# Weight-block sums by adding DMAs, another order of the seven products, and no arithmetic on GpSimd

## Chip, cores and metric

One core of one Trainium2 chip runs the whole program. The metric is device time in microseconds of one execution of the program, as the median of several runs. The profile is of one execution.

## The reference, cut to what matters

Two encoder layers on 512 tokens of width 1024: latent attention in the first, grouped-query attention in the second, each beside a four-head cross-attention into 256 memory tokens, an output projection with residual, and then a SwiGLU block:

```python
def _swiglu(h, w_gate_up, w_down):
    gu = h @ w_gate_up                       # (512, 1024) @ (1024, 2 * 2816)
    g, u = gu[..., :D_FF], gu[..., D_FF:]
    return (jax.nn.silu(g) * u) @ w_down

for i in range(DEPTH):
    ...
    x = x + jnp.concatenate([mix, mem_out], axis=-1) @ w_out[i]
    x = x + _swiglu(_rmsnorm(x, norm_ffn[i]), w_gate_up[i], w_down[i])
```

All weights and activations are float32.

## The kernel before

**Products in three passes.** Every large product is made of float32r matmuls. A weight tile is loaded in float32 (`load_raw`, L166, from SyncE's queue), ACT rounds it to a high half (`whi`, L154 in `wsplit`), DVE subtracts to get the low half (`wlo`, L155), and `mm3` (L137 to L139) issues three matmuls: high by high, high by low, low by high. An activation tile is split in the same way.

**Gate/up in seven products instead of eight** (`ffn`). The reduction (1024) is cut in two halves, the tokens in two halves, and a group of columns holds gate columns and the up columns that belong to them. So a group has four weight blocks: B11 and B21 (gate, upper and lower half of the reduction), B12 and B22 (up), numbered q = 0, 2, 1, 3. Seven products P1 to P7 of sums of A blocks (activations) by sums of B blocks (weights) replace the eight plain ones. There are six groups a layer, five 512 columns wide (each block two tiles of 128x1024) and a last one 256 wide (each block one tile). A step is one weight tile of one product: twelve matmuls of 512 moving columns, so a full group has 14 steps.

The list `PROD` sets the order of products. `prep(g, p, i)` makes the weight tile of a step; `ahead(n)` calls it two steps ahead of the matmuls (`LW=2`), and the high and low halves lie in three buffers each (`WF=3`). In `prep`, the function `tadd` subtracts in place on DVE (L793): two subtractions for each tile of P7, one for P6, one for P4, so 8 of 128x1024 in a full group. `post(g, p)` takes a product out of PSUM: ACT copies for P1, P7 and P5 (L868, L872, L880), GpSimd adds P7 to P5 (L881) and P6 to that (L886), DVE does the rest (L885, L890, L892, L896, L897). `act_T` transposes a group's result for w_down after the next group's P1. The A sums (`get` in `w_out`, L708) are made once a layer, when the first group needs them.

**w_down** (after the groups): each activation tile is split by ACT (`ah`, L943) and, by turns, DVE and GpSimd (`al`, L944, `wlod='VP'`).

**Elsewhere on GpSimd**: `rope_tables` loads tables with DMAs from GpSimd's queue (L375, L376, L380) and multiplies them there (L386, L387), at the start of the program and at the start of layer 1.

**Order.** The program is written in one order, and a scheduler places each engine's instructions and inserts the semaphore waits. Each engine, and each queue, runs its list in order.

Of the kernel before, what the change touches and what calls it, by code (L numbers as in the profile page):

```python
# [28 lines left out]

CFG = dict(mid=3, mgap=3, mdel=7, warm=9, npre=(3, 3), pre=(6, 5), WC=512, mm=3, sc=3, tp=2, norm='VA', G=33, T=9,  # L30
           W=7, WH=6, WF=3, RF=3, PR=4, delay=12, ssq='AV', ahead=1, gtag=('sc', 'mm', 'mm', 'mm'), LA=3, wlos='V',
           wloa='V', wlof='V', wlod='VP', scl='V', rm='V', rad='V', hi='A', rawe='A', LW=2, tadd='V',
           r=(0.534, 0.925, 0.95, 5, 1.124, 0.86, 1.362))
# [15 lines left out]
def encoder_kernel(ctx: ExitStack, tc: tile.TileContext, a: dict, out: bass.AP):  # L49
# [270 lines left out]
    def w_early(src, n):  # L320

        ws = []
        raw = g4(dt=F32, name="raw")
        nc.sync.dma_start(raw[:, : n * 512], src[:, : n * 512])
        for i in range(n):
            w = pair()
            split(w, raw[:, i * 512 : (i + 1) * 512])
            ws.append(w)
        return ws
# [39 lines left out]
    def rope_tables(cs, rows, row0, d, ntab):  # L369
        t_cs = gt((P, 2, 4, d), F32) if 8 * d <= 512 else None  # L370
        if t_cs is None:
            t_c, t_s = [x.rearrange("p (t d) -> p t d", t=4) for x in pair(F32)]
        else:
            t_c, t_s = t_cs[:, 0], t_cs[:, 1]
        GP.dma_start(t_c, cs[0].rearrange("p (t d) -> p t d", t=4))  # L375
        GP.dma_start(t_s, cs[1].rearrange("p (t d) -> p t d", t=4))  # L376
        out = []
        for i in range(ntab):
            g = tt()[:, : 2 * d]
            GP.dma_start(g, rows[:, row0 + 2 * i * d : row0 + (2 * i + 2) * d])  # L380
# [6 lines left out]
            GP.tensor_mul(sg, t_s, g[:, d : 2 * d].unsqueeze(1).to_broadcast([P, 4, d]))  # L387
            out.append((cg, sg))
        return out
# [293 lines left out]

    def w_out(l, acts, banks, pre, X, g0, early):

# [18 lines left out]
        def sums(x, y, op):  # L704
# [4 lines left out]
            return o  # L709

        def get(name):
            (a11, a21), (a12, a22) = rows
# [4 lines left out]
            if name == "A12":  # L717
                scale_rows(1)
                return operand(a12)
            if name == "S1":  # L720
                tmp["S1"] = sums(a21, a22, V.tensor_add)
                return operand(tmp["S1"])
            if name == "S2":
                tmp["S2"] = sums(tmp["S1"], a11, V.tensor_sub)
                return operand(tmp["S2"])
            if name == "A22":
                return operand(a22)
            return operand(sums(a12, tmp["S2"], V.tensor_sub))

# [8 lines left out]
        for i, (c, kp, ts) in enumerate(steps):  # L738
# [17 lines left out]
            elif (c, kp) == (1, 3):  # L756
                scale_rows(0)
        add_x(X, 1, bs[1], sq, range(4))

        def stats():  # L760
            tot = small(4, "sqt")
            V.tensor_add(tot, sq[:, :4], sq[:, 4:])
            return token_rstd(tot, 4, D, f"rf{l}")[0]

# [3 lines left out]

    PROD = ["P1", "P7", "P2", "P5", "P6", "P4", "P3"]
    AOP = dict(P1="A11", P7="S3", P2="A12", P5="S1", P6="S2", P4="A22", P3="S4")  # L770

    def ffn(l, X, acts, banks, pre, g0, emit):
# [11 lines left out]
        def ntile(g):  # L784
            return 2 if g < 5 else 1

        def load_q(g, q):
            if g < NG:
                src = [a["w_gu"][l, g, q, i] for i in range(2)] if g < 5 else [a["w_gl"][l, q]]
                raws[g, q] = [load_raw(x, 1024) for x in src]  # L790

        def tadd(o, x, y):
            (V if eng("tadd") == "V" else GP).tensor_sub(o, x, y)  # L793

        def prep(g, p, i):
            b11, b12, b21, b22 = [raws[g, q][i] if (g, q) in raws else None for q in range(4)]
            if p == "P1":
                src = b11
            elif p == "P7":
                tadd(b11, b12, b11)  # L800
                tadd(b12, b22, b12)
                src = b12
            elif p == "P2":
                src = b21
            elif p == "P5":
                src = b11
            elif p == "P6":
                tadd(b11, b22, b11)
                src = b11
            elif p == "P4":  # L810
                tadd(b11, b21, b11)
                src = b11
            else:
                src = b22
            return wsplit(src, 1024, "wlof")

# [4 lines left out]
        def ahead(n):  # L821
            while nprep[0] < min(n, len(steps)):
# [16 lines left out]
        def early(get):  # L839
            if getop[0] is None:  # L840
                getop[0] = get
                load_q(0, 0)
                ahead(1)
            else:
                ahead(2)

        stats = w_out(l, acts, banks, pre, X, g0, early)
        st = {}
# [14 lines left out]
        def post(g, p):  # L863
# [5 lines left out]
            elif p == "P7":  # L869
                st["p7"] = two()  # L870
                for t in range(2):
                    A.copy(st["p7"][t][:, :n], st["B"][t])  # L872
            elif p == "P2":
                st["gs"] = [pr(), pr()]
                for t in range(2):
                    A.activation(st["gs"][t][:, :n], st["A"][t], AF.Silu, scale=r[:, t : t + 1])
            elif p == "P5":
                st["p5"] = two()
                for t in range(2):
                    A.copy(st["p5"][t][:, :n], st["C"][t])  # L880
                    GP.tensor_add(st["p5"][t][:, :n], st["p5"][t][:, :n], st["p7"][t][:, :n])  # L881
            elif p == "P6":
                for t in range(2):
                    w, z = st["p1"][t][:, :n], st["p5"][t][:, :n]
                    V.tensor_add(w, st["D"][t], w)  # L885
                    GP.tensor_add(z, z, w)  # L886
            elif p == "P4":
                for t in range(2):
                    w, z, q = [st[x][t][:, :n] for x in ("p1", "p5", "p7")]
                    V.tensor_add(q, st["B"][t], w)  # L890
                    A.activation(q, q, AF.Silu, scale=r[:, 2 + t : 3 + t])
                    V.scalar_tensor_tensor(z, z, r[:, 2 + t : 3 + t], q, ALU.mult, ALU.mult)  # L892
            else:
                for t in range(2):
                    w, q = st["p1"][t][:, :n], st["gs"][t][:, :n]
                    V.tensor_add(w, st["C"][t], w)  # L896
                    V.scalar_tensor_tensor(w, w, r[:, t : t + 1], q, ALU.mult, ALU.mult)  # L897
                return [st["p1"][0], st["p1"][1], st["p5"][0], st["p5"][1]]

# [602 lines left out]
```

## Time and profile before

| | us |
|---|---|
| median of 3 runs | 1308.55 (1307.23 to 1310.11) |
| the profiled execution | 1308.39 |
| its span in the trace | 1306.6 |
| TensorE matmul busy | 1273.2 |
| DVE busy | 945.6 |
| ACT busy | 711.7 |
| GpSimd busy | 155.9 |
| read from HBM | 119.24 MB |

The profile shows engines as PE (TensorE's matmuls), PEld (its weight loads), DVE, ACT, POOL (GpSimd) and SP (SyncE); a q behind a name is the engine's queue or sequencer. L155 is a line of the kernel before. Matmuls are pipelined: 0.39 us is the time of one from its start to its end, while the next begins earlier. The 1.8 us between the profiled execution's time and its span lie around the instructions.

### The profile page before, as it was taken

What the parts mean: (1) busy time and instruction counts of PE and PEld (TensorE: products, weight loads), DVE (VectorE), ACT (ScalarE), POOL (GpSimd) and SP (SyncE); (2) the same over time, 40 slices, a digit from 0 to 9 for tenths busy, and PEclk for the clock granted to TensorE, in tenths of its full rate; (3) what the DMA queues carried; (4) which work ended last, traced back from release to release, by engine and by line L of the source; (5) the groups of instructions that cost most, each with busy time, mean ns of one, the idle gap of its engine ahead of it and who ended that gap; (6) DMA issues with size and microseconds to landing.
All of it is one profiled execution on the core that took longest, in us unless ns stands there. A gap on an engine that the chain in (4) does not pass through costs nothing. (4 is left out here: it accounts for less than half of the span.)

```text
span 1306.6 us, 17197 instructions
## 1 busy us (share of the span) xinstructions
PE 1273.2 (97%) x6425; PEld 1063.0 (81%) x6425; DVE 945.6 (72%) x1591; ACT 711.7 (54%) x1229; POOL 155.9 (12%) x84
## 2 busy tenths in 40 slices
PE   8999999989999999989999999999999999999998
PEld 6988878878878887978888888887887888898887
DVE  6699998735987988962326798965498888888221
ACT  5587776834755455542324478866375555555110
POOL 2000000000312221330100000000013222035000
PEclk9999999989999999999999999999999999999999
DMA  6342101053233231241313212223304133215210
GB/s 224 116 139 85 34 1 49 1 209 113 78 132 129 81 121 46 76 165 49 125 49 113 89 49 70 77 81 113 113 34 176 55 123 113 79 52 186 106 62 33
DMA packets 45027, 122.44 MB, mean 94 GB/s; under 512 B 5217, under 2 KB 9825, under 8 KB 44945
## 3 DMA queue, kind: packets, MB, share of 16 engines
q1 hardware_dynamic: 44352, 119.58, 26.7%
q0 software_dynamic: 592, 1.77, 0.4%
q8 instruction: 50, 0.82, 0.3%
q14 instruction: 33, 0.26, 0.1%
HBM read 119.24 MB, written 2.10 MB: 93 GB/s over the span
## 5 line engine op out<-in xcount | busy, mean ns | idle before, releaser
L155 DVE TENSOR_TENSOR wlo<-raw,whi 128x1024 fp32r<-128x1024 f32 (+3 forms) x342 | 375.3, 1106 | 248.0 <-ACT whi L154 246.1
L154 ACT CAST whi<-raw 128x1024 fp32r<-128x1024 f32 (+3 forms) x342 | 299.2, 885 | 394.0 <-PE sc L139 259.1
L881 POOL TENSOR_TENSOR t<-t,t 128x512 f32<-128x512 f32 (+1 forms) x24 | 65.1, 2733 | 901.1 <-ACT t L880 901.1
L137 PE MATMUL mm<-whi,g 128*128 128x512 f32 (+3 forms) x370 | 141.6, 384 | 1.2 <-ACT whi L154 1.2
L138 PE MATMUL mm<-wlo,g 128*128 128x512 f32 (+3 forms) x370 | 139.8, 378 | 0.5 <-DVE wlo L155 0.5
L139 PE MATMUL mm<-whi,g 128*128 128x512 f32 (+3 forms) x370 | 138.8, 378 | 0.0
L138 PE MATMUL mm<-wlo,op 128*128 128x512 f32 (+1 forms) x336 | 127.3, 379 | 4.3 <-DVE wlo L155 3.8
L137 PE MATMUL mm<-whi,op 128*128 128x512 f32 (+1 forms) x336 | 125.9, 375 | 3.2 <-ACT whi L154 3.2
L139 PE MATMUL mm<-whi,op 128*128 128x512 f32 (+1 forms) x336 | 125.9, 375 | 0.0
L139 PE MATMUL sc<-whi,op 128*128 128x512 f32 (+1 forms) x336 | 125.1, 372 | 0.0
L138 PE MATMUL sc<-wlo,op 128*128 128x512 f32 (+1 forms) x336 | 125.0, 372 | 0.0
L137 PE MATMUL sc<-whi,op 128*128 128x512 f32 (+1 forms) x336 | 124.9, 372 | 0.0
L793 DVE TENSOR_TENSOR raw<-raw,raw 128x1024 f32<-128x1024 f32 x88 | 110.5, 1275 | 1.1
L138 PEld LDWEIGHTS mm<-wlo,op 128*128 128x128 f32 x336 | 63.2, 188 | 21.9 <-DVE wlo L155 11.3
L137 PEld LDWEIGHTS mm<-whi,g 128*128 128x128 f32 x370 | 69.8, 189 | 12.5 <-ACT whi L154 1.6
L138 PEld LDWEIGHTS mm<-wlo,g 128*128 128x128 f32 x370 | 70.2, 190 | 10.5 <-DVE wlo L155 1.0
L139 PEld LDWEIGHTS mm<-whi,g 128*128 128x128 f32 x370 | 69.8, 189 | 10.9 <-DVE g L246 0.2
L137 PEld LDWEIGHTS mm<-whi,op 128*128 128x128 f32 x336 | 63.3, 188 | 14.7 <-ACT whi L154 3.6
L499 PE MATMUL sc<-g,g 128*128 128x512 f32 x256 | 73.6, 403 | 0.6 <-ACT g L243 0.6
L138 PE MATMUL mm<-wlo,ah 128*128 128x512 f32 x176 | 69.0, 392 | 4.3 <-DVE wlo L155 4.3
L138 PEld LDWEIGHTS sc<-wlo,op 128*128 128x128 f32 x336 | 63.3, 188 | 11.2
L139 PEld LDWEIGHTS sc<-whi,op 128*128 128x128 f32 x336 | 63.3, 188 | 11.0
(243 smaller groups left out, 2663.6 us busy)
## 6 DMA issues: line engine op xcount, KB each, us to landing
raw<-in_w_gu SPq DMA_DIRECT2D x80, 512.0 KB, 4.3
raw<-in_w_dn SPq DMA_DIRECT2D x44, 512.0 KB, 3.9
raw<-in_w_out SPq DMA_DIRECT2D x24, 512.0 KB, 4.4
raw<-in_w_mkv SPq DMA_DIRECT2D x32, 256.0 KB, 2.9
raw<-in_w_gin SPq DMA_DIRECT2D x30, 256.0 KB, 3.0
raw<-in_w_gl SPq DMA_DIRECT2D x8, 512.0 KB, 4.0
raw<-in_w_out SPq DMA_DIRECT2D x12, 256.0 KB, 2.5
raw<-in_w_qb SPq DMA_DIRECT2D x12, 192.0 KB, 2.3
```

What stands on the lines that cost most here:

```text
L137: PE.matmul(out, lhi, rhi, start=start, stop=False, skip_group_check=skip)
L138: PE.matmul(out, lhi, rlo, start=False, stop=False, skip_group_check=skip)
L139: PE.matmul(out, llo, rhi, start=False, stop=stop, skip_group_check=skip)
L154: A.copy(hi[:, :n], raw)
L155: (V if eng(kind) == "V" else GP).tensor_sub(lo[:, :n], raw, f(hi[:, :n]))
L499: PE.matmul(sc, lq[:, q * P : (q + 1) * P], rk, start=i == 0, stop=i == len(passes) - 1)
L793: (V if eng("tadd") == "V" else GP).tensor_sub(o, x, y)
L881: GP.tensor_add(st["p5"][t][:, :n], st["p5"][t][:, :n], st["p7"][t][:, :n])
```

## The change

- **Weight sums.** The seven products get signs so that each B sum is a plain addition. The subtractions on DVE (`tadd`, L793) go. In their place GpSimd's queue issues DMAs that read a weight block from HBM a second time and add it into the tile in SBUF (`add_q`, L808 of the new kernel). Tile q = 0 is split for P1, then B12 is added into it and it is split for P5, then B22 (split for P6), then B21 (split for P4). Tile q = 1 gets B22 added before it is split for P7. That is 8 adding DMAs of 512 KB in a full group and 4 in the last group, 88 in all.
- **Order of products.** P1, P7, P5, P2, P6, P3, P4 instead of P1, P7, P2, P5, P6, P4, P3. So the splits of tile q = 0 lie four steps apart (steps 0, 4, 8, 12 of the 14). The A sums change signs to match, and the third product of a layer is S1 (two sums, then splits) instead of A12.
- **Loads.** All loads of the second to fourth block go to the `raw` buffers (four instead of three), those of q = 0 to the general pool (32 slots instead of 33). The first group's loads start two steps of w_out earlier (`first`).
- **GpSimd's arithmetic goes.** The P5 sum is one DVE instruction that reads PSUM (instead of an ACT copy and a GpSimd addition), the P6 sum, all of w_down's `al` and the rope tables' multiplications move to DVE.
- `w_early` loads two tiles of 512 columns apart instead of one of 1024.

```diff
-    ..., G=33, ... RF=3, ... wlod='VP', ...
+    ..., G=32, ... RF=4, ... wlod='V', ...
...
-            GP.tensor_mul(cg, t_c, g[:, :d].unsqueeze(1).to_broadcast([P, 4, d]))
+            V.tensor_mul(cg, t_c, g[:, :d].unsqueeze(1).to_broadcast([P, 4, d]))
...
-    PROD = ["P1", "P7", "P2", "P5", "P6", "P4", "P3"]
+    PROD = ["P1", "P7", "P5", "P2", "P6", "P3", "P4"]
...
+        def add_q(g, q, by, i):
+            if g < NG:
+                GP.dma_start(raws[g, q][i], w_src(g, by)[i], accum_op=ALU.add)
+
+        BOP = dict(P1=(0, 1), P7=(1, None), P5=(0, 3), P2=(2, None), P6=(0, 2), P3=(3, None), P4=(0, None))
+
+        def load_sum(g):
+            load_q(g, 1)
+            for i in range(ntile(g) if g < NG else 0):
+                add_q(g, 1, 3, i)
+
         def prep(g, p, i):
-            b11, b12, b21, b22 = [raws[g, q][i] if (g, q) in raws else None for q in range(4)]
-            if p == "P1":
-                src = b11
-            elif p == "P7":
-                tadd(b11, b12, b11)
-                tadd(b12, b22, b12)
-                src = b12
-...
+            q, by = BOP[p]
+            w = wsplit(raws[g, q][i], 1024, "wlof")
+            if by is not None:
+                add_q(g, q, by, i)
+            return w
...
                 if i == 0:
-                    for q in {"P1": [1, 3], "P7": [2], "P5": []}.get(p, []):
-                        if (g, q) not in raws:
-                            load_q(g, q)
-                    if p == "P6":
+                    if p == "P5":
+                        load_q(g, 2)
+                    elif p == "P2":
+                        load_q(g, 3)
+                    elif p == "P6":
                         load_q(g + 1, 0)
-                    if p == "P3":
-                        load_q(g + 1, 1)
+                    elif p == "P3":
+                        load_sum(g + 1)
...
             elif p == "P5":
                 st["p5"] = two()
                 for t in range(2):
-                    A.copy(st["p5"][t][:, :n], st["C"][t])
-                    GP.tensor_add(st["p5"][t][:, :n], st["p5"][t][:, :n], st["p7"][t][:, :n])
+                    V.tensor_add(st["p5"][t][:, :n], st["C"][t], st["p7"][t][:, :n])
             elif p == "P6":
                 for t in range(2):
                     w, z = st["p1"][t][:, :n], st["p5"][t][:, :n]
                     V.tensor_add(w, st["D"][t], w)
-                    GP.tensor_add(z, z, w)
+                    V.tensor_add(z, z, w)
```

**GpSimd, one full group of layer 0** (`t` are results of products, `raw` weight tiles). Before, the four additions of two tiles each:

```order
L881 TENSOR_TENSOR t_1175_5071<-t_1175_5071,t_1159_4991 128x512
L881 TENSOR_TENSOR t_1176_5072<-t_1176_5072,t_1160_4992 128x512
L886 TENSOR_TENSOR t_1175_5071<-t_1175_5071,t_1145_4927 128x512
L886 TENSOR_TENSOR t_1176_5072<-t_1176_5072,t_1146_4928 128x512
```

Now, tile q = 0 being `raw_1119` and `raw_1120`, and `raw_1189` and `raw_1190` being the next group's q = 1:

```order
L808 DMA raw_1119_4727<-in_w_gu 128x1024
L808 DMA raw_1120_4729<-in_w_gu 128x1024
L808 DMA raw_1119_4727<-in_w_gu 128x1024
L808 DMA raw_1120_4729<-in_w_gu 128x1024
L808 DMA raw_1189_5085<-in_w_gu 128x1024
L808 DMA raw_1119_4727<-in_w_gu 128x1024
L808 DMA raw_1190_5087<-in_w_gu 128x1024
L808 DMA raw_1120_4729<-in_w_gu 128x1024
```

The list holds the additions for P5, P6 and P4 of both tiles, and the next group's sums stand between those for P4, on the same queue.

**DVE around a change of groups in layer 0.** Before, from the last product but one (`mm`, `sc` are PSUM):

```order
L892 SCALAR_TENSOR_TENSOR t_1176_5072<-t_1176_5072,rf0_975_4017,t_1160_4992 128x512
L793 TENSOR_TENSOR raw_1169_5033<-raw_1183_5117,raw_1169_5033 128x1024
L155 TENSOR_TENSOR wlo_1194_5180<-raw_1170_5035,whi_1193_5179 128x1024
L896 TENSOR_TENSOR t_1145_4927<-mm_1167_5031,t_1145_4927 128x512
L896 TENSOR_TENSOR t_1146_4928<-sc_1168_5032,t_1146_4928 128x512
L897 SCALAR_TENSOR_TENSOR t_1145_4927<-t_1145_4927,rf0_975_4017,pr_1165_5027 128x512
L897 SCALAR_TENSOR_TENSOR t_1146_4928<-t_1146_4928,rf0_975_4017,pr_1166_5028 128x512
L793 TENSOR_TENSOR raw_1183_5117<-raw_1189_5159,raw_1183_5117 128x1024
L793 TENSOR_TENSOR raw_1170_5035<-raw_1184_5119,raw_1170_5035 128x1024
L155 TENSOR_TENSOR wlo_1200_5208<-raw_1183_5117,whi_1199_5207 128x1024
```

Now, the same place (the last product is P4, L907 and L909):

```order
L155 TENSOR_TENSOR wlo_1202_5166<-raw_1179_5041,whi_1201_5165 128x1024
L155 TENSOR_TENSOR wlo_1204_5183<-raw_1180_5043,whi_1203_5182 128x1024
L907 TENSOR_TENSOR t_1167_4995<-mm_1159_4955,t_1151_4925 128x512
L907 TENSOR_TENSOR t_1168_4996<-sc_1160_4956,t_1152_4926 128x512
L155 TENSOR_TENSOR wlo_1208_5208<-raw_1189_5085,whi_1207_5207 128x1024
L909 SCALAR_TENSOR_TENSOR t_1177_5037<-t_1177_5037,nr0_978_4025,t_1167_4995 128x512
L909 SCALAR_TENSOR_TENSOR t_1178_5038<-t_1178_5038,nr0_978_4025,t_1168_4996 128x512
L155 TENSOR_TENSOR wlo_1210_5224<-raw_1190_5087,whi_1209_5223 128x1024
```

The first low half of P7 (`wlo_1200` before, `wlo_1208` now) has three subtractions of 128x1024 fewer between it and the end of the old group, and stands ahead of that group's last two instructions.

## Rows read from the trace of the kernel before

**Rows 1.** Windows: gate/up of layer 0, its end, gate/up of layer 1 (stretch and length, busy, clock, DMA share, GB/s).

```profile
340.00:560.00 220.00, 214.66 (x1055) 178.58 (x1054) 192.05 (x185) 123.00 (x161) 55.30 (x25) 1.00 0.30 101
560.00:580.00 20.00, 16.30 (x65) 12.97 (x64) 17.73 (x9) 10.79 (x12) 12.99 (x5) 0.91 0.33 120
960.00:1180.00 220.00, 217.05 (x1062) 180.98 (x1062) 190.99 (x186) 127.17 (x168) 55.08 (x25) 1.00 0.27 94
```

**Rows 2.** Waits of weight loads, 340 to 560 us (who waited for whom: total, times, longest).

```profile
PEld mm L138 <- DVE wlo L155: 6.5, 11, 1.1
PEld mm L137 <- ACT whi L154: 2.1, 1, 2.1
```

**Rows 3.** The same, 960 to 1180 us.

```profile
PEld mm L138 <- DVE wlo L155: 4.9, 10, 1.0
PEld mm L137 <- ACT whi L154: 1.5, 1, 1.5
```

**Rows 4.** The same, 1180 to 1200 us.

```profile
PEld mm L138 <- DVE wlo L155: 1.1, 1, 1.1
```

**Rows 5.** The same, first 30 us.

```profile
PEld sc L139 <- DVE wlo L155: 1.4, 2, 1.2
PEld mm L139 <- DVE wlo L155: 1.1, 2, 0.8
```

**Rows 6.** Timeline of PE where w_down begins, layer 0 (start, duration, instruction, idle before).

```profile
565.19 0.39 PE L137 MATMUL sc<-whi,ah 128*128 128x512 f32 x1
...
566.55 0.39 PE L137 MATMUL mm<-whi,ah 128*128 128x512 f32 x1
570.64 0.50 PE L138 MATMUL mm<-wlo,ah 128*128 128x512 f32 x1 [3.70 <-DVE wlo L155]
...
572.03 0.63 PE L139 MATMUL mm<-whi,al 128*128 128x512 f32 x1
572.46 0.63 PE L137 MATMUL sc<-whi,ah 128*128 128x512 f32 x1
```

**Rows 7.** Timeline of DVE, the same place.

```profile
561.25 6.04 DVE L944 TENSOR_TENSOR al<-at,ah 128x1024 fp32r<-128x1024 f32 x2 [0.67 <-ACT ah L943]
567.21 6.68 DVE L155 TENSOR_TENSOR wlo<-raw,whi 128x1024 fp32r<-128x1024 f32 x2
```

**Rows 8.** Timeline of POOL, the same place.

```profile
560.35 12.46 POOL L944 TENSOR_TENSOR al<-at,ah 128x1024 fp32r<-128x1024 f32 x4 [7.26 <-ACT ah L943]
```

**Rows 9.** Line L155 from 340 to 560 us: duration ns least/median/most.

```profile
L155 DVE TENSOR_TENSOR wlo<-raw,whi x73: 1207/1224/2315, 339.3 to 553.1; 128x1024 fp32r<-128x1024 f32 x73
```

**Rows 10.** Groups of DVE, 340 to 560 us (busy us, mean ns, idle before).

```profile
L155 DVE TENSOR_TENSOR wlo<-raw,whi 128x1024 fp32r<-128x1024 f32 x73 | 99.7, 1383 | 23.7 <-ACT whi L154 23.2
L793 DVE TENSOR_TENSOR raw<-raw,raw 128x1024 f32<-128x1024 f32 x40 | 52.8, 1342 | 0.4
...
L885 DVE TENSOR_TENSOR t<-mm,t 128x512 f32<-128x512 f32 x5 | 3.4, 678 | 0.0
```

**Rows 11.** Line L380, DMAs issued by POOL: time of the issue, ns.

```profile
L380 POOL DMA_DIRECT2D t<-in_rows x4: 534/536/582, 3.8 to 619.9; - x4
```

**Rows 12.** Group of ACT over the span: the high half (busy us, mean ns, idle before).

```profile
L154 ACT CAST whi<-raw 128x1024 fp32r<-128x1024 f32 x220 | 230.0, 1053 | 328.7 <-PE sc L139 211.8 <-DVE raw L793 52.5 <-PE mm L139 34.1
```

**Rows 13.** The profile page, DMA issues (count, KB each, median us from issue to landing).

```profile
raw<-in_w_gu SPq DMA_DIRECT2D x80, 512.0 KB, 4.3
...
g<-in_rope_mla POOLq DMA_DIRECT2D x2, 256.0 KB, 6.2
...
g<-in_rope_gqa POOLq DMA_DIRECT2D x2, 256.0 KB, 2.9
```

**Rows 14.** DMA queues from 400 to 500 us (packets, MB, share of 16 engines).

```profile
q1 hardware_dynamic: 2796, 10.14, 28.9%
```

**Rows 15.** The chain that ended last: one instruction in two groups of layer 1, two groups apart.

```profile
1034.77 1.13 DVE raw L793
...
1115.85 1.13 DVE raw L793
```

More of the change, by code (lines that the diff above doesn't have):

```diff
@@ L322, in w_early @@
         ws = []
-        raw = g4(dt=F32, name="raw")
-        nc.sync.dma_start(raw[:, : n * 512], src[:, : n * 512])
         for i in range(n):
-            w = pair()
-            split(w, raw[:, i * 512 : (i + 1) * 512])
-            ws.append(w)
+            raw, hi, lo = tt(), tt(dt=F32R), tt(dt=F32R)
+            nc.sync.dma_start(raw, src[:, i * 512 : (i + 1) * 512])
+            split((hi, lo), raw)
+            ws.append((hi, lo))
         return ws
@@ L682, in add_x, with w_out @@
             A.activation(tt(), xc, AF.Square, accum_out=sq[:, 4 * c + t : 4 * c + t + 1])
-    def w_out(l, acts, banks, pre, X, g0, early):
+    def w_out(l, acts, banks, pre, X, g0, first, early):
         sq = small(8, f"sq{l}", bufs=1)
@@ L727, in get @@
                 return operand(a22)
-            return operand(sums(a12, tmp["S2"], V.tensor_sub))
+            return operand(sums(tmp["S2"], a12, neg_sum))
         n = len(banks)
@@ L757, in w_out @@
                 scale_rows(0)
+                first()
         add_x(X, 1, bs[1], sq, range(4))
@@ L845, in early, with first @@
                 ahead(2)
-        stats = w_out(l, acts, banks, pre, X, g0, early)
+        def first():
+            load_q(0, 0)
+            load_sum(0)
+        stats = w_out(l, acts, banks, pre, X, g0, first, early)
         st = {}
@@ L872, in post @@
                     A.copy(st["p7"][t][:, :n], st["B"][t])
+            elif p == "P5":
+                st["p5"] = two()
+                for t in range(2):
+                    V.tensor_add(st["p5"][t][:, :n], st["C"][t], st["p7"][t][:, :n])
             elif p == "P2":
@@ L875, in post @@
                 for t in range(2):
[L876 to L879, printed above, removed]
-                    A.copy(st["p5"][t][:, :n], st["C"][t])
-                    GP.tensor_add(st["p5"][t][:, :n], st["p5"][t][:, :n], st["p7"][t][:, :n])
+                    A.activation(st["gs"][t][:, :n], st["A"][t], AF.Silu, scale=r[0][:, t : t + 1])
             elif p == "P6":
@@ L885, in post @@
                     V.tensor_add(w, st["D"][t], w)
-                    GP.tensor_add(z, z, w)
-            elif p == "P4":
+                    V.tensor_add(z, z, w)
+            elif p == "P3":
+                st["p3"] = [pr(), pr()]
+                for t in range(2):
+                    w, q, u = [st[x][t][:, :n] for x in ("p1", "gs", "p3")]
+                    V.tensor_add(u, st["C"][t], w)
+                    V.scalar_tensor_tensor(u, u, r[1][:, t : t + 1], q, ALU.mult, ALU.mult)
+            else:
                 for t in range(2):
@@ L890, in post @@
                     V.tensor_add(q, st["B"][t], w)
[L891 to L898, printed above, removed]
+                    A.activation(q, q, AF.Silu, scale=r[0][:, 2 + t : 3 + t])
+                    V.scalar_tensor_tensor(z, z, r[1][:, 2 + t : 3 + t], q, ALU.mult, ALU.mult)
+                return [st["p3"][0], st["p3"][1], st["p5"][0], st["p5"][1]]
         BANK = dict(P1="A", P7="B", P2="A", P5="C", P6="D", P4="B", P3="C")
```

46 lines of the change are left out of this document (20 added, 26 removed).

## Prediction

> **What bounds the kernel now.** I first cut the span into stages. In gate/up of layer 0 TensorE is busy 214.66 of 220 us, in layer 1 217.05 of 220; DVE is busy 192.05 and 190.99 there, so nearly nine tenths, and GpSimd a quarter [rows 1]. TensorE sets the time, and DVE is the engine that sometimes keeps it waiting. So the change can give back only what TensorE loses, and the next view is who it waits for. Its weight loads wait for low and high halves of weights: 6.5 and 2.1 us in layer 0 [rows 2], 4.9 and 1.5 us in layer 1 [rows 3], 1.1 us where layer 1 goes over to w_down [rows 4], 1.4 and 1.1 us at the program's start [rows 5]. Where layer 0 goes over to w_down, two matmuls start 4.09 us apart (566.55 and 570.64) and the trace names `wlo`; afterwards matmuls start 0.43 us apart instead of 0.23 [rows 6]. The granted clock of that stretch is 0.91 [rows 1]: after the idle gap it fell to 1.2 GHz, and that is 9% of 20 us, 1.8 us more.
>
> Why is `wlo` late? In the last place DVE spends 6.04 us on two `al` and 6.68 us on two `wlo` [rows 7], while GpSimd works on four `al` for 12.46 us [rows 8]. A `wlo` alone takes 1.22 us (median), the longest 2.3 us [rows 9]. So the two engines slow each other, and over gate/up of layer 0 the mean is 1.38 us [rows 10]. The second reason is DVE's own list: 40 subtractions of weight blocks, 52.8 us in five groups [rows 10], stand between the splits.
>
> **What leaves and what comes on the engines.** A full group loses 8 subtractions of 1.34 us on DVE, 10.7 us [rows 10]. It gains four instructions of 512 columns there (the sums for P5 and P6), about 0.68 us each by the row of a like one [rows 10], 2.7 us. If the 73 splits also fall from 1.38 to 1.22 us [rows 9, 10], DVE saves 12 us more over the stretch. So its 192 us become about 192 - 53 + 14 - 12 = 141 of 220. w_down's eleven `al` that move from GpSimd cost DVE about 1.22 us each (priced as a `wlo` of the same size [rows 9]); DVE waits for work in w_down, and the four that lie at the change of stage take the place of two that were stretched to 3 us each. The eight multiplications of the rope tables, 0.68 us each at most, cost DVE under 3 us at each of two starts; in layer 1 they stand behind four splits that are ahead of need, so I cost them at nothing, and at the program's start I keep 1 us for them. The ACT copies for P5 go; ACT is not what is waited for. `w_early` moves the same bytes: nothing.
>
> **What TensorE can get back.** From above, all these waits: 8.6 (layer 0) + 3.9 + 1.8 (end of layer 0, 4.09 less one normal 0.23, and the clock) + 6.4 (layer 1) + 1.1 + 2.5 (start) = 24.3 us [rows 1 to 6]. From below, TensorE's plain idle time by the windows, 5.3 + 3.7 + 2.9, and the clock: 13.8 us [rows 1]; it counts too little, because a matmul's busy time of 0.39 us covers the start of a gap. I take, stage by stage, 6.5 of 8.6, 5 of 5.7, 4.5 of 6.4, 0.5 of 1.1 and 1.5 of 2.5: 18 us. What stays is at the changes of groups, where transposes and ends of products still meet. Against it stand two things. The third product's A sums (two more additions of 0.68 us ahead of it [rows 10]) come where a layer's first group already keeps DVE full: 0 to 2.8 us for both layers, I take 2. And adding DMAs that come a little late: 0 to 23 us (below), I take 1.5. The sum is -14.5 us.
>
> **The adding DMAs.** This is the unknown: no row of before shows one. GpSimd's part is small, an issue takes 0.54 us [rows 11], 4.3 us in a group. What matters is whether the four steps between two splits of tile q = 0 are enough. A step is twelve matmuls 0.227 us apart (565.19 to 566.55 are six), 2.72 us [rows 6]. A split starts when TensorE frees its buffer, two steps ahead, and takes 1.05 us on ACT [rows 12] and 1.22 us on DVE [rows 9]. So the addition has 4 x 2.72 - 2.3 = 8.6 us before the next split of the tile is held back, and TensorE itself stands only after two steps less one split, 3.1 us, more: 11.7 us. A plain load of 512 KB lands after 4.3 us [rows 13]. Of that its bytes take 1.49 us of all 16 DMA engines (10.14 MB take 28.9% of 100 us [rows 14]). An addition in place has to read the tile as well as the block, so I count its bytes twice: 2.98 us, landing after 5.8 us. That is inside 8.6. The tightest place is where the next group's two sums stand between the additions for P4 on GpSimd's queue: four additions in about two steps, so the last may land some 3.5 us later, 9.3 us, late for its split but not for TensorE. The far ends: no dearer than a load, 4.3 us; or twice the 6.2 us that 256 KB from GpSimd's queue took in the crowded first microseconds [rows 13], 12.4 us. At that end TensorE waits 0.7 us at three places in a group, 2.1 us, and with ten full groups and two small ones 23 us. I take 5.8, near the plain load, because only the bytes grow.
>
> The Trainium skill, "Collectives: The Full Stack", section "The bandwidth ceiling: the fold count and why AG ≠ RS ≠ AR", puts a DMA that adds at two reads for each write and gives measured rates in the ratio 1.93. By it an addition would take an estimated 2.9 us of the engines, and the sum would stay as it is. No run here shows it yet.
>
> Total rate: a group lasts 40.5 us (81.08 us for two [rows 15]). Eight loads take 11.9 us of the DMA engines and eight additions 23.8, 88% of it. The share was 0.27 to 0.30 [rows 1].
>
> **Sum.** The profiled execution took 1308.39 us, the median is 1308.55, so the two may stand for each other. 1308.4 - 14.5 = **1294 us**. A measurement of this kernel can tell about 0.2%, 2.6 us, from no change.
>
> **The rivals.**
>
> *A. The additions saturate the DMA engines (slower).* It decides where an addition costs more than 2.4 times a load: then (1 + 2.4) x 11.9 us is the whole 40.5 us of a group. At three times, a group needs 47.7 us, 7.1 more; ten full groups and two half ones make 78 us, so about 1372 us. For it: the additions double what is read, and a load that came late 88 times over has nowhere to hide. Against it: 0.88 leaves room, and loads of the other blocks have several steps of lead. The Trainium skill, "DMA: Bandwidth & Descriptors", section "Issuing engines are not separate DMA queues", says that DMAs of all queues run on the same 16 engines; the 6.2 against 2.9 us for 256 KB from GpSimd's queue at a crowded and a quiet time [rows 13] agrees. Were they apart, a group would be full only at 3.4 times. Chance 0.18.
>
> *B. The additions keep up in rate but land late.* Near the far end above, 12.4 us: 23 us in place of the 1.5 counted, 1294 - 1.5 + 23 = 1315 us. For it: loads and additions come in bursts. Against it: the 3.1 us that the split's own lead still covers. Chance 0.08.
>
> *C. The waits change their name.* DVE is relieved but TensorE still waits at each change of groups, now for the transposes' copies, and at the third product of each layer, so that only the end of layer 0 (5.7) and the start (1.5) are won, less 2: 1308.4 - 5.2 = 1303 us. For it: a change of groups has a chain of PSUM, DVE, ACT and TensorE that no spare time on DVE shortens. Against it: the waits of weight loads above 1 us are all for the two halves of weights [rows 2 to 5]. Chance 0.12.
>
> **How the numbers follow.** The forecast (additions in time) has 0.62 and gives 1284 (all 24.3 us) to 1302 us; with C, and B but for its worst, the range 1284 to 1316 holds 0.80. A lies outside. Faster by over 0.2%: the forecast's 0.62, most of C (0.10) and some of B (0.02), 0.74. Within 0.2%: 0.05. Slower: A, and the rest of B, 0.21.
>
> **What the profile would show.** Right: no subtraction of weight blocks on DVE, splits at 1.2 us throughout, DVE near 65% busy in gate/up, no clock below full at the start of w_down, the DMA share there near 0.8 to 0.9, and TensorE's waits for `wlo` in gate/up under 3 us a layer. Each addition should land after 5 to 7 us. Wrong by A: a DMA share at its ceiling, and ACT's high halves waiting for GpSimd's DMAs in every group. Wrong by B: the same wait, but for P6's and P4's splits alone, with DMA engines idle between. Wrong by C: waits of transposes in place of those for `wlo`.

## The result, and the profile after

The changed kernel is slower by 0.8%. Its median is 1321.19 us (1318.42 to 1323.55, 6 runs) against 1309.42 us (1307.23 to 1314.33, 6 runs) of the kernel before on the same chip: ratio 1.0082, 95% interval 1.0059 to 1.0105. The forecast was 1294 us, the range ended at 1316.

The page of the changed kernel, engines and DMA queues (busy us, share of the span, instructions; packets, MB, share of 16 engines):

```profile
PE 1289.2 (98%) x6425; PEld 1061.6 (80%) x6425; DVE 838.0 (64%) x1572; ACT 699.6 (53%) x1205; POOL 83.6 (6%) x105
q1 hardware_dynamic: 44784, 119.58, 25.6%
q0 software_dynamic: 13264, 47.91, 19.9%
```

DVE and GpSimd lost what they were to lose (945.6 and 155.9 us before). q1 has the loads, q0 the adding DMAs and GpSimd's few tables. Windows of the changed kernel (stretch, length, busy of PE, PEld, DVE, ACT, POOL, clock, DMA share, GB/s); the last three answer to [rows 1]:

```profile
240.00:260.00 20.00, 20.00 (x148) 18.51 (x147) 16.07 (x42) 18.73 (x52) 0.00 (x0) 1.00 0.29 97
260.00:280.00 20.00, 20.00 (x96) 16.41 (x95) 9.95 (x13) 8.19 (x15) 0.00 (x0) 1.00 0.70 279
340.00:560.00 220.00, 210.17 (x1011) 170.49 (x1011) 134.60 (x158) 110.29 (x140) 31.64 (x36) 1.00 0.74 182
560.00:580.00 20.00, 20.00 (x88) 16.22 (x87) 14.94 (x13) 12.96 (x14) 0.00 (x0) 1.00 0.58 206
960.00:1180.00 220.00, 212.65 (x986) 171.45 (x985) 140.64 (x161) 116.48 (x148) 34.96 (x40) 1.00 0.77 189
```

The end of layer 0 came as forecast: TensorE is busy for 20.00 us and at full clock, where it had 16.30 us and 0.91. But in gate/up it is busy less than before (210.17 us against 214.66 in layer 0), although DVE has been relieved there. The waits of ACT in the changed kernel, whole span (who waited for what: us in all, times, longest):

```profile
ACT whi L154 <- DMA raw<-in_w_gu: 38.7, 9, 6.5
ACT whi L154 <- DMA raw<-in_w_gl: 12.7, 6, 3.8
```

51.4 us in 15 waits: ACT's rounding of a weight tile now waits for a DMA, and these are the adding ones. The line of the additions (the time of an issue in ns, least/median/most; who waited for them; the time from issue to landing, when the data are in the tile):

```profile
L808 POOL DMA_DIRECT2D raw<-in_w_gu x80: 866/875/1948, 282.8 to 1148.0; - x80
...
  ACT whi L154: 51.4, 15
...
DMA to landing us min/median/max: 5.0/6.3/14.2
```

A second loss shows in no wait. Timeline of PE in w_down of the changed kernel, which the change does not touch but for `al`:

```profile
619.22 0.39 PE L137 MATMUL mm<-whi,ah 128*128 128x512 f32 x1
...
621.08 0.39 PE L139 MATMUL sc<-whi,al 128*128 128x512 f32 x1
```

The same place in the kernel before:

```profile
619.33 0.39 PE L138 MATMUL mm<-wlo,ah 128*128 128x512 f32 x1
...
621.14 0.39 PE L137 MATMUL mm<-whi,ah 128*128 128x512 f32 x1
```

From the first to the last start there are eight matmuls in 1.86 us, 0.2325 us each, where the kernel before needed 1.81 us, 0.226 us each. The granted clock from 600 to 680 us is 1.00 in both. The program has 4369 matmuls of 512 columns. Over all that follow one another without a stop the mean is 0.2277 us before and 0.2324 us now; 4.7 ns on each make some 20 us. (The expectations below count 5.7 ns on each, 25 us, from w_down alone; that is too much.)

So there are two losses to explain, late additions and slower matmuls, and a gain that the forecast had not counted: between 240 and 280 us TensorE no longer stands.

### The profile page after: what moved, and what is told of

The parts are those of the page before. It is cut to its first block, busy times and chain, and to the rows that moved or that the text cites. A ratio compares the mean times of both kernels' runs of the same rounds, so it can differ in the third digit from the quotient of the medians.

```text
span 1319.2 us, 17231 instructions
## 1 busy us (share of the span) xinstructions
PE 1289.2 (98%) x6425; PEld 1061.6 (80%) x6425; DVE 838.0 (64%) x1572; ACT 699.6 (53%) x1205; POOL 83.6 (6%) x105
## 3 DMA queue, kind: packets, MB, share of 16 engines
q1 hardware_dynamic: 44784, 119.58, 25.6%
q0 software_dynamic: 13264, 47.91, 19.9%
## 5 line engine op out<-in xcount | busy, mean ns | idle before, releaser
L155 DVE TENSOR_TENSOR wlo<-raw,whi 128x1024 fp32r<-128x1024 f32 (+3 forms) x342 | 345.1, 1013 | 350.3 <-ACT whi L154 349.4
L137 PE MATMUL mm<-whi,op 128*128 128x512 f32 (+1 forms) x336 | 128.8, 383 | 5.6 <-ACT pr L892 3.1
L808 POOL DMA_DIRECT2D raw<-in_w_gu x80 | 70.3, 949 | 889.8 <-DMA raw<-in_w_gu 589.2
L139 PE MATMUL mm<-whi,op 128*128 128x512 f32 (+1 forms) x336 | 126.6, 377 | 0.0
L137 PEld LDWEIGHTS mm<-whi,op 128*128 128x128 f32 x336 | 63.2, 188 | 23.0 <-ACT pr L892 8.1
L139 PEld LDWEIGHTS mm<-whi,g 128*128 128x128 f32 x370 | 69.5, 188 | 11.7
L498 PE MATMUL sc<-g,g 128*128 128x512 f32 x256 | 75.1, 410 | 0.7 <-ACT g L243 0.6
L139 PEld LDWEIGHTS sc<-whi,op 128*128 128x128 f32 x336 | 63.3, 188 | 12.3
L137 PEld LDWEIGHTS sc<-whi,op 128*128 128x128 f32 x336 | 63.3, 188 | 12.2
L139 PEld LDWEIGHTS mm<-whi,op 128*128 128x128 f32 x336 | 63.3, 189 | 11.6
```

The lines of the kernel that those rows point to most:

```text
L137: PE.matmul(out, lhi, rhi, start=start, stop=False, skip_group_check=skip)
L139: PE.matmul(out, llo, rhi, start=False, stop=stop, skip_group_check=skip)
L155: (V if eng(kind) == "V" else GP).tensor_sub(lo[:, :n], raw, f(hi[:, :n]))
L498: PE.matmul(sc, lq[:, q * P : (q + 1) * P], rk, start=i == 0, stop=i == len(passes) - 1)
L808: GP.dma_start(raws[g, q][i], w_src(g, by)[i], accum_op=ALU.add)
```

## The experiments

Ratios are to the kernel before on the same chip, with 95% intervals.

### Is it the chip, the pools' sizes, or the additions?

The kernel before and the changed kernel, unchanged, went to one chip together, with two more: the kernel before with the changed sizes of its pools, and the changed kernel without its adding DMAs (it then multiplies by weight blocks where sums should stand).

```diff
-G=33, ... RF=3
+G=32, ... RF=4
```

```diff
-                GP.dma_start(raws[g, q][i], w_src(g, by)[i], accum_op=ALU.add)
+                pass
```

> The kernel before, unchanged, to see the spacing of its matmuls on the chip that the next three run on. In the first profiles, matmuls of 512 columns in w_down of layer 0 (600 to 676 us) start 0.2267 us apart before and 0.2324 us after the change, and so everywhere in the program. Theory P (a property of the changed program): 0.2267 here, about 1308 us. Theory C (the chip or the execution): 0.232 here, about 1330 us.

> The changed kernel, unchanged, on the same chip. Theory P: 0.2324 us spacing again and about 1320 us. Theory C: the same spacing as the run of the kernel before on this chip, whatever it is; then about 1297 us if that is 0.2267 (its stalls are 7 us fewer).

> The kernel before with the pools' sizes of the changed one alone (32 general slots instead of 33, four raw buffers instead of three). If where tiles lie in SBUF sets the spacing (one form of theory P): 0.232 us and about 1308 + 4369 x 0.0057 = 1333 us. If not: 0.2267 us and 1305 to 1312 us.

> The changed kernel without its 88 adding DMAs, so that products use weight blocks in place of their sums; all else stays. If the adding DMAs cost TensorE its time (waits in gate/up, or the spacing): under 1300 us. If they cost nothing and the rest of the change does: about 1320 us, spacing 0.232 us.

Measured: the kernel before 1310.4 us with matmuls 0.227 us apart; the changed kernel 1327.01 us, 1.0131 (1.0103 to 1.0158), 0.232 us; the sizes alone 1307.66 us, 0.998 (0.9966 to 0.9993), 0.227 us; without the additions 1301.06 us, 0.9933 (0.9918 to 0.9948), still 0.232 us (under 1300 us had been expected if the additions cost the time, about 1320 if not). So the spacing belongs to the program, not to the chip, and comes neither from the two sizes nor from the additions. The additions cost 26 us. The changed kernel itself is half a percent slower on this chip than on the first (1.0131 against 1.0082), so a difference of that size between chips says little.

### Where the weight tiles lie

The changed kernel has two new small tiles, `nr0` and `nr1` (64 bytes a partition each), in a pool that is laid out ahead of the weight pool. By the addresses of the built programs, the kernel before has every moving tile of its 512-column matmuls a multiple of 256 bytes away from the stationary one; in the changed kernel 4032 of the 4369 are an odd multiple of 128 away. The other 337 are a control inside the same program: 256 of them, the matmuls of attention scores (L498), have both tiles in one pool, and they keep their start-to-start time, 0.231 us in the mean against 0.230 before. The next kernels move tiles by 128 bytes: the changed kernel's weights, the weights of the kernel before, those of the changed kernel without additions, and all tiles of the kernel before.

```diff
-    sp.tile([P, 16], F32, tag="pad", name="pad", bufs=1)
+    sp.tile([P, 48], F32, tag="pad", name="pad", bufs=1)
```

```diff
     sp.tile([P, 16], F32, tag="pad", name="pad", bufs=1)
+    cp.tile([P, 32], F32, tag="low", name="low")
```

> The changed kernel with one edit: the pad tile of the pool of small tiles is 128 bytes a partition longer, so that every tile of the weight pool lies 128 bytes higher and its address again differs from those of the activation tiles by a multiple of 256 bytes, as in the kernel before (in the changed kernel the two new small tiles nr0 and nr1 moved the weight pool by 128). Theory (the place of the weight tiles against the activation tiles sets the spacing of the 512-column matmuls): spacing 0.227 us again in place of 0.232, 4369 matmuls x 5.7 ns = 25 us less than the changed kernel: ratio to the kernel before 0.994 (0.990 to 0.998), the late adds stay. Rival 1 (the spacing comes from the idle GpSimd, that is from arithmetic that no longer runs there): spacing 0.232, ratio 1.010. Rival 2 (the spacing comes from the order of the products or the w_early tiles): the same 1.010.

> The kernel before with the same 128 bytes added to its pad tile, nothing else: its weight tiles then differ from the activation tiles by an odd multiple of 128 bytes, as in the changed kernel. Theory of the addresses: spacing 0.232 us, ratio 1.015 to 1.020 (25 us of spacing, less what its waits for weight halves take up, at most 5 us). Rivals (idle GpSimd, order of products): nothing moves, spacing 0.227, ratio 1.000.

> The changed kernel with the 128 bytes and without the 88 adding DMAs (the products then use weight blocks in place of sums of blocks). Theory of the addresses: the 1301 us of the changed kernel without adds, less 25 us of spacing: ratio 0.974 (0.970 to 0.980), and that is the floor of the change with its adds for nothing. Rivals (idle GpSimd, order): ratio 0.993 as without the 128 bytes.

> The kernel before with a tile of 128 bytes in the first pool, so that activation tiles and weight tiles both lie 128 bytes higher: each now begins at an odd multiple of 128, and they still differ by a multiple of 256. Theory A (what counts is where the moving tile lies against the stationary one): spacing 0.227 us, ratio 1.000. Theory B (what counts is that the moving tile itself begins at a multiple of 256): spacing 0.232 us, ratio 1.011 as with the weight tiles alone moved.

The same place in w_down, kernel before with its weights moved by 128 bytes:

```profile
619.32 0.39 PE L137 MATMUL sc<-whi,ah 128*128 128x512 f32 x1
...
621.18 0.39 PE L139 MATMUL mm<-whi,al 128*128 128x512 f32 x1
```

Kernel before with all tiles moved (its lines stand one lower):

```profile
619.29 0.39 PE L139 MATMUL sc<-wlo,ah 128*128 128x512 f32 x1
...
621.10 0.39 PE L138 MATMUL mm<-whi,ah 128*128 128x512 f32 x1
```

Changed kernel with its weights moved:

```profile
619.41 0.39 PE L137 MATMUL mm<-whi,ah 128*128 128x512 f32 x1
...
621.22 0.39 PE L139 MATMUL sc<-whi,al 128*128 128x512 f32 x1
```

Eight matmuls each: 1.86 us, then 1.81 and 1.81. Weights alone moved: 1324.12 us, 1.0114 (1.0097 to 1.0131). All moved: 1310.89 us, 0.9996 (0.9979 to 1.0012). So 128 unused bytes cost the kernel before 1.1%. Expected were 1.5 to 2.0%, from the 25 us; of the 20 us that the spacing makes, waits took up some: by the pages TensorE's time without a matmul falls from 33.4 to 30.3 us. What counts is where the moving tile lies against the stationary one, not where it begins: theory A holds. An idle GpSimd or the order of products has no part in it, since the kernel before has the old ones and becomes slow by the 128 bytes alone.

In the changed kernel without additions the 128 bytes give back 1.4% (1281.62 us, 0.9789, 0.9775 to 0.9804). With the additions they give little or nothing: 1320.42 us, 1.0085 (1.007 to 1.010), where the changed kernel had 1.0082 and 1.0131 on two other chips. That is a clear miss of the expectation of 0.994, though the matmuls are faster. Waits of ACT in that run:

```profile
ACT whi L154 <- DMA raw<-in_w_gu: 59.5, 16, 6.8
ACT whi L154 <- DMA raw<-in_w_gl: 11.7, 4, 3.4
```

These are 71.2 us, where the two profiles of the changed kernel have 51.4 and 62.1: ACT waits 9 to 20 us more for the same DMAs. The mean granted clock of the execution is 0.992, where those two have 0.999 and 0.994, and that is 3 to 9 us. So what the faster matmuls gave went into longer waits and into the clock; how it divides is not settled. That the landing of the additions sets the pace while they are late is tested next, by landing them in time.

### The order of the additions

The changed kernel's queue, in its burst of four (timeline of POOL: start, duration, instruction, idle before), and how that burst lands (line L808, 422 to 427 us):

```profile
422.56 3.58 POOL L808 DMA_DIRECT2D raw<-in_w_gu  x4 [8.17 <-DMA raw<-in_w_gu]
```

```profile
L808 POOL DMA_DIRECT2D raw<-in_w_gu x4: 875/1341/1470, 422.6 to 424.7; - x4
...
  ACT whi L154: 8.9, 2
...
DMA to landing us min/median/max: 5.2/9.8/14.2
```

The scheduler had put the next group's sums between the two additions for P4, and the queue first waits 8.17 us for the load that the first sum needs. Four stand in a row. The first lands 5.2 us after its issue at 422.6 us, the last 14.2 us after its own at 424.7 us, so 11 us behind the first, and it is one for P4. ACT waits 8.9 us for two of the four. The next kernels put the sums behind the additions for P4, with the 128 bytes and without them:

```diff
+                last[0] = GP.dma_start(raws[g, q][i], w_src(g, by)[i], accum_op=ALU.add).ins
...
+                    with tc.issue_after(last[0]):
                         add_q(g, 1, 3, i)
```

> The changed kernel with the 128 bytes, and the two adds that make the next group's P7 sum issued behind the last add of the group's q = 0 tiles instead of between them. In the trace of the changed kernel the burst of four adds lands one after the other, 3 us apart, and the second P4 tile's add, the last of the four, lands 13 us after its issue: ScalarE's cast waits 5 us for it in four groups of five. Theory (the adds are late where four of them stand in a row, by their order): those waits fall to under 1 us, and 15 to 25 us of the 26 us that the adds cost come back: ratio 0.978 to 0.985. Rival (the adds are late because they and the loads fill the DMA engines): the wait moves to P7's sum or to P5's adds, and the ratio stays within 0.003 of the run with the 128 bytes alone.

> The changed kernel with the order of the adds alone (the next group's sums behind the last add of the q = 0 tiles), without the 128 bytes. With the 128 bytes this order gave a ratio of 0.988, and the 128 bytes alone gave nothing (1.0085). Theory (two causes in one place: while the adds are late, the landing of the adds sets the pace and a faster TensorE only waits longer; with the adds in order TensorE sets it again): spacing 0.232 us, and 18 to 22 us more than with both, as between the two runs without adds (1301 and 1282): ratio 1.002 to 1.006. Rival (the order alone is all that mattered): ratio 0.988 to 0.991.

The burst with 128 bytes and the new order, timeline of POOL and line L808 from 417 to 424 us:

```profile
417.87 0.87 POOL L808 DMA_DIRECT2D raw<-in_w_gu  x1 [7.29 <-DVE wlo L155]
420.59 2.67 POOL L808 DMA_DIRECT2D raw<-in_w_gu  x3 [1.85 <-DVE wlo L155]
```

```profile
who waited for it (us, times):
busy tenths in 40 slices 0000000000000100000000000000000000000000
DMA to landing us min/median/max: 5.5/7.6/12.8
```

The last still lands after 12.8 us, but it is a sum that has time, and nobody waits. 1293.72 us, 0.988 (0.9865 to 0.9895): 27 us better than the 128 bytes alone on the same chip, all that the additions had been thought to cost, and faster than the kernel before. (The expected 0.978 to 0.985 started from a run that had itself been expected lower.) The order alone: 1312.22 us, 1.0001 (0.999 to 1.0013), a little better than expected. So the 128 bytes give little or nothing while the additions are late and 1.2% once they are in order; the order gives 0.8 to 1.3% by itself and 2.0% on top of the 128 bytes. The work of the DMA engines is the same and only its order differs: their share from 340 to 520 us is 0.80 in the changed kernel and 0.83 with both edits.

### What is left of the additions, and what they are worth

With both cures TensorE still stood in the last group of each layer. There the splits of the tile q = 0 lie two steps apart. First the four sums of that group went to DVE; then all sums (with four buffers for blocks two to four, and with six).

```diff
+            if g == 5 and by is not None:
+                V.tensor_add(raws[g, 0][0], raws[g, 0][0], raws[g, by][0])
-            if by is not None:
+            elif by is not None:
```

```diff
-                GP.dma_start(raws[g, q][i], w_src(g, by)[i], accum_op=ALU.add)
+            V.tensor_add(raws[g, q][i], raws[g, q][i], raws[g, by][i])
```

> The run with the 128 bytes and the order of the adds, and in the last group of each layer (256 columns, one tile a block) the four sums made by DVE from blocks loaded once instead of by adding DMAs. In that group the splits of the q = 0 tile lie two steps apart, 5.8 us, and an add lands 5.3 us after an issue that itself waits for the split, so ScalarE waits 2 to 3 us for it; TensorE stands 6.3 us in all between 520 and 560 us and 6.5 us between 1140 and 1180 us. Theory (the adds are late there by their latency, not by the load on the DMA engines): these fall to 1 to 2 us a layer, 8 to 10 us gained: ratio 0.980 to 0.983. Rival (DVE's additions, four of 1.3 us a layer, come late too, as in the kernel before): 0 to 4 us gained, ratio 0.985 to 0.988.

> The changed kernel with the 128 bytes and with every sum of weight blocks made by DVE (additions in place, 8 of 128x1024 in a full group) from blocks that are loaded once; order of products, signs, the missing arithmetic on GpSimd all as in the changed kernel. No adding DMA is left. Theory (the adding DMAs, once they land in time, take 40 additions of 1.34 us a layer from DVE, and DVE's halves then come in time): DVE is back at over 70% in gate/up, TensorE waits for weight halves at P7 and P6 again as in the kernel before (some 5 us a layer): ratio 0.981 to 0.987. Rival (what gained was the order of products, the earlier loads and GpSimd's arithmetic, the adding DMAs gave nothing): ratio 0.975 to 0.979, as with the last group alone on DVE (0.9767). Rival 2 (four buffers hold the blocks too long and loads come late): ratio over 0.990.

> The same with six buffers for the second to fourth block (and 30 slots in place of 32 in the general pool), so that no load waits for a buffer. Theory (DVE's halves are late): within 0.002 of the run with four buffers. Rival 2 (buffers): 0.005 or more below it.

Windows of gate/up, last group on DVE:

```profile
340.00:560.00 220.00, 219.38 (x1080) 183.44 (x1080) 153.48 (x172) 120.39 (x149) 26.42 (x30) 1.00 0.75 186
960.00:1180.00 220.00, 219.38 (x1080) 183.28 (x1079) 149.95 (x168) 118.96 (x147) 26.43 (x30) 1.00 0.74 189
```

All sums on DVE, four buffers:

```profile
340.00:560.00 220.00, 218.01 (x1072) 181.11 (x1071) 191.52 (x207) 120.60 (x150) 0.00 (x0) 1.00 0.34 110
960.00:1180.00 220.00, 218.05 (x1071) 180.96 (x1071) 188.65 (x203) 117.82 (x146) 0.00 (x0) 1.00 0.33 112
```

Last group on DVE: 1282.31 us, 0.9767 (0.9752 to 0.9783), the fastest of the kernels that make all sums, and better than expected. All sums on DVE: 1286.0 us, 0.9817 (0.9796 to 0.9838); with six buffers 1286.14 us, 0.9819, so four buffers cost nothing. The adding DMAs, in time, are worth 0.5% by the ratios, whose intervals do not touch, and 3.7 us by the medians of the two chips: TensorE is busy 2.7 us more over the two stretches, and DVE has 38 us less to do in each. The expectation had it that without adding DMAs TensorE would wait some 5 us a layer; by the windows it stands 2 us in each, against 0.6.

### The edits beside the sums

All sums on DVE is still 23 us faster than the kernel before. Two small edits were made alone in the kernel before: the low halves of w_down's activations all on DVE, and the new `w_early`; then both.

```diff
-           wloa='V', wlof='V', wlod='VP', ...
+           wloa='V', wlof='V', wlod='V', ...
```

```diff
-        raw = g4(dt=F32, name="raw")
-        nc.sync.dma_start(raw[:, : n * 512], src[:, : n * 512])
         for i in range(n):
-            w = pair()
+            raw, hi, lo = tt(), tt(dt=F32R), tt(dt=F32R)
+            nc.sync.dma_start(raw, src[:, i * 512 : (i + 1) * 512])
```

> The kernel before with one letter changed: the low halves of w_down's activation tiles all on DVE, none on GpSimd. In the kernel before TensorE stands 5.7 us at 565 us behind GpSimd's 12.46 us for one such tile, and the clock falls for 3.4 us. Theory (the forecast's term for the end of layer 0): 5 us gained at layer 0 and about half a microsecond at layer 1: ratio 0.996 (0.9945 to 0.997). Rival (DVE's queue takes the wait over): under 2 us, ratio 0.9985 to 1.000.

> The kernel before with the new form of w_early alone (two tiles of 512 columns from the pool of small tiles, three of 512 each, in place of one of 1024 and two pairs from the general pool). In the kernel before nothing is loaded from 240 to 260 us (1 GB/s); SyncE's queue starts the loads of w_out at 260.46 us, and TensorE stands 6.4 us between 240 and 280 us, with the clock at 0.83 of full in the second half of it. In the changed kernel the loads run by 250.57 us, and TensorE stands nowhere there. Theory (the early weights wait for a slot of the general pool, and all loads behind them on SyncE's queue with them; the forecast took this edit for nothing): that stop goes, 6.4 us and 3.4 us of clock: ratio 0.9925 (0.990 to 0.995). Rival (what took the stop away is the space that other edits left in the general pool, or the earlier first loads): ratio 0.998 to 1.001.

> The kernel before with the new w_early and with all low halves of w_down's activations on DVE, two small edits that have nothing to do with sums of weights. The second alone gave 0.9916. Theory (the two places are far apart, so the gains add): ratio 0.984 (0.981 to 0.987), which is nearly all that the changed kernel gains with all its sums on DVE (0.9817). Rival (they share a clock fall or a wait): ratio 0.988 to 0.992.

The kernel before, windows, then SyncE's queue there (its wait from 215 to 262 us and two rows of its timeline; L324 is the load of the early tile), then a row of ACT and one of PE:

```profile
240.00:260.00 20.00, 18.22 (x135) 16.47 (x133) 16.29 (x42) 18.61 (x52) 0.00 (x0) 1.00 0.00 1
260.00:280.00 20.00, 15.35 (x59) 11.88 (x58) 5.98 (x8) 4.18 (x7) 0.00 (x0) 0.83 0.80 315
```

```profile
SPq L166 <- DVE wlo L155: 46.6, 1, 46.6
...
260.46 0.33 SPq L166 DMA_DIRECT2D raw<-in_w_out  x1
260.85 0.42 SPq L324 DMA_DIRECT2D raw<-in_w_out  x1
...
265.37 1.14 ACT L249 CAST g<-raw 128x512 fp32r<-128x512 f32 x2 [2.19 <-DMA raw<-in_w_out]
266.04 0.79 PE L137 MATMUL mm<-g,g 128*128 128x512 f32 x1 [3.48 <-ACT g L249]
```

With `w_early` alone (L325 are the loads of the early tiles):

```profile
240.00:260.00 20.00, 20.00 (x147) 18.44 (x145) 16.03 (x44) 18.71 (x53) 0.00 (x0) 1.00 0.09 26
260.00:280.00 20.00, 20.00 (x97) 16.85 (x96) 9.47 (x11) 7.69 (x14) 0.00 (x0) 1.00 0.69 278
```

```profile
203.80 2.26 SPq L325 DMA_DIRECT2D t<-in_w_out  x2
...
257.11 0.80 SPq L166 DMA_DIRECT2D raw<-in_w_out  x2
```

The stop of 6.4 us (1.78 and 4.65) and the fall of the clock in that stretch are gone: 1298.12 us, 0.9914 (0.9885 to 0.9944). The size is as expected, but the rows show another way than the theory's. In the kernel before the queue stands 46.6 us in front of another load of `w_out` (L166), until DVE has made a `wlo`. The early tile's load comes right behind it, ACT waits for it until 265.37 us, and TensorE stands 3.48 us until ACT has split that tile. In the new form the early loads go out 57 us sooner, ahead of that load. What the other 2.9 us of the stop hung on stays open.

The letter `wlod` alone: 1301.53 us, 0.9916 (0.990 to 0.9932), 10.5 us where 5.5 had been expected (the 12.46 us of GpSimd that the expectation names are four tiles, not one [rows 8]). The windows show 3.7 us and 1.8 us of clock at 560 us and 0.9 us at 1180 us (19.08 us busy of 20, then 20.00). The profiled executions of the two kernels lie only 7.1 us apart (1308.39 and 1301.28); the median of the kernel before on this chip is 1312.0 us, at a mean clock of 0.991 where its profile has 0.994. So the windows account for most of what the profiles differ by, and the rest of the 10.5 us is not located.

Both: 1290.66 us, 0.9864 (0.983 to 0.9898). The theory's 0.984 lies inside that interval, the rival's 0.988 too, so whether the two simply add is not settled. They make some 18 of the 23 us.

## Why the prediction was wrong, by its own steps

- **The price of an addition** was right. "I count its bytes twice: 2.98 us, landing after 5.8 us". From 400 to 500 us of the changed kernel:

```profile
q0 software_dynamic: 2592, 9.44, 51.9%
q1 hardware_dynamic: 2696, 9.86, 25.9%
```

  9.44 MB are 18 additions, 2.88 us of the 16 engines each; a byte costs 2.09 times one of a load here, and 1.94 times over the program (19.9% for 47.91 MB, 25.6% for 119.58). The earliest landing of an addition is 5.0 us after its issue; the eight of the last groups take 5.3 us (median). The rule of the Trainium skill ("Collectives: The Full Stack", section "The bandwidth ceiling: the fold count and why AG ≠ RS ≠ AR"), two reads for each write, is given there for the adding step of collectives; its measured ratio of 1.93 agrees with these figures. Rival A, DMA engines full over a whole group, did not happen: the share in gate/up was 0.74 to 0.77, and 0.85 with the order mended did no harm. In a burst they are nearly full: 0.87 from 427 to 440 us of the changed kernel.

- **The step that failed first**: "four additions in about two steps, so the last may land some 3.5 us later, 9.3 us, late for its split but not for TensorE". The place was right, the size was not. The additions of a burst land one after another, 2.6 to 5.0 us apart by their packets: the fourth lands 11 us behind the first and 14.2 us after its issue, past the 11.7 us at which TensorE stands. The forecast took 1.5 us for lateness. It cost 26 us by taking the additions away at 0.232 us a matmul, and 39 us (1320.42 less 1281.62) at 0.227; of these the order alone gave back 27. That is rival B (0.08), in its place, at more than its price of 23 us. A second part of the step: the 8.6 us were worked out from four steps between two splits, and used for every group. In the last group of a layer there are two, so by the same sum 3.1 us, and an addition that lands after 5.3 us is late for its split even by itself: ACT waits six times, 2.1 us in the mean (12.7 us). With those sums on DVE the time is some 11 us less (1293.72 less 1282.31, on two chips).

- **What no step had**: the addresses. Two small tiles of 64 bytes that the forecast did not look at made 4032 of the 512-column matmuls longer, some 20 us in all. That is 14.7 us in the kernel before (1324.12 less 1309.37) and 1.4% between the two kernels without additions.

- **"`w_early` moves the same bytes: nothing"** was wrong by 10.6 us in the other direction. The bytes were the same, the place of the loads in SyncE's queue was not. The forecast looked for weight halves that came late and never cut out the stretch from 240 to 280 us, where TensorE waits for a load.

- **What TensorE gets back in gate/up and at its end** was right in mechanism. DVE falls to 134.6 us (141 was forecast; the stretch holds 4% fewer matmuls than before), the low half takes 1.22 us again:

```profile
L155 DVE TENSOR_TENSOR wlo<-raw,whi 128x1024 fp32r<-128x1024 f32 x70 | 85.4, 1224 | 82.0 <-ACT whi L154 81.9
```

  and with the additions in time and the last group's sums on DVE TensorE's idle time in the two stretches falls from 5.3 and 2.9 us [rows 1] to 0.62 and 0.62. That is 7 us by the windows, where the forecast took 11 from the waits. The end of layer 0 was put at 5 us; its windows show 5.5, and the run of that letter alone gave 10.5 by the medians.

- **The sum**: forecast 1294. The changed kernel with 128 bytes and the additions in order takes 1293.72 us, but that is chance: it holds the 10.6 us of `w_early`, which the forecast put at nothing, and lateness in the last group takes about as much back.

## What to carry to other kernels

Read the trace for every stop of the engine that sets the time, not only for stops of the kind that the change is aimed at: two of the larger gains here were a load that stood behind another load's wait in a queue, and a letter. Where DMAs that depend on each other share a queue, cost the burst, not the mean rate: the last of four in a row is the one that counts, so put the one with the nearest due time first and look in the built order whether it stayed there. And when a change adds a tile, compare the start-to-start time of matmuls in a stretch that it does not touch; if that moved, look at addresses before looking at waits.

## What the hardware showed that was not expected

- A 512-column matmul in float32r starts 0.2325 us after the one before it where its moving tile and its stationary tile differ by an odd multiple of 128 bytes, 0.226 to 0.227 us where they differ by a multiple of 256, both in w_down with the granted clock at 1.00. Other distances were not tried, and why it is so is open. The kernel before shows the slower spacing too, for some ten matmuls after a stop (timeline of PE, kernel before):

```profile
384.08 0.40 PE L139 MATMUL mm<-whi,op 128*128 128x512 f32 x1
...
386.41 0.39 PE L137 MATMUL mm<-whi,op 128*128 128x512 f32 x1
...
388.67 0.39 PE L138 MATMUL sc<-wlo,op 128*128 128x512 f32 x1
```

  Ten in 2.33 us, then ten in 2.26 us. Here it settles; with the other distance it is still 0.2325 us in w_down, in a stretch without a stop.
- The issue of an adding DMA takes GpSimd 0.875 us, against 0.534 us for a plain one [rows 11], by which the forecast had priced it.
- A faster TensorE gave little while it waited for late DMAs: the 128 bytes were worth 0 to 0.5% with late additions and 1.2% with additions in order.
